# Other banks for the second token block, another order of the first drains, and two transposing chains a tick later

## The chip, the cores and the metric

The kernel runs on one core of a Trainium2 chip. The metric is the device time of one execution in microseconds (us), here the median of 3 runs. The engines are PE (TensorE), DVE (VectorE), ACT (ScalarE), POOL (GpSimd) and SP (SyncE), which issues the transfers. Each has one queue and goes through it in the order of the program; where an instruction waits, all behind it on that engine wait too.

## What is computed

A trunk of two layers over 256 tokens of width 1024, all in float32. Cut to what matters here:

```python
for l in range(2):
    x = x + 0.5 * swiglu(rms_norm(x), w1, w3, w2)          # inner width 2816
    z = rms_norm(x) @ w_in                                 # 1024 -> 6752 columns
    y_na  = neighborhood_attention(norm(na_q), norm(na_k), na_v, bias)
    y_gla = gla_bidirectional(gq, gk, gv, log_sigmoid(gfl @ up_f), log_sigmoid(gbl @ up_b))
    y_mla = softmax_attention(q from c_q, k and v from c_kv, rotary part)   # 4 heads, dense
    m = sum(sigmoid(gate_i) * (y_i @ w_br_i) for the three branches)
    x = x + m @ w_out
    x = x + 0.5 * swiglu(rms_norm(x), w1, w3, w2)
```

## The kernel before

Every float32 operand of a weight product is kept as a high and a low part in a rounded 32-bit format, and a product is three matmuls (high x high, high x low, low x high). The weights come as 212 units of up to 1 MB, in the order of use: SP brings a unit into one of three raw buffers, ACT writes its high half (L138), DVE the low half (L144), each in two pieces, into one of four buffers `hl`; then PE uses it. Products run one unit after the other, and the two token blocks of 128 tokens (t = 0 and 1) share each unit.

Two mechanisms set the order of everything. The first is `tick()`, called between bursts of matmuls: it emits the pending weight splits (`fill`) and then one step of each spawned task whose countdown has run out, in the order in which they were spawned. `spawn(gen, wait)` sets that countdown; a task is a generator, and where it yields it gives way until a later tick. So a `wait` of 1 or 2 shifts all steps of that task against the bursts, and against the steps of the other tasks, on all engines. The second is the banks of PSUM: `acc_t` gives one of four accumulator banks, `at_t` and `tr_t` one of four others (names beginning with ta); the bank released longest ago is given out first, and the first writer waits until its last reader is done.

What the change touches:

- `ffn`, the feed-forward stage, two per layer. `fform(i)` makes unit i of the first product: 32 matmuls into two acc banks, which `fdrain` empties: ACT L480 and DVE L481 add the two halves, POOL L482 multiplies by the norm's factor, ACT L487 is the Silu, DVE L489 the product, ACT L491 and DVE L493 split it. In layer 0's first stage the first two units were computed at the start, ahead of the norm's factor; they are emptied later by DVE L485 and L486, straight with the factor, at i == FIRST_R (2).
- `wide_out(first, lhs, nu, done)` is the second product, and w_out's in the mixer: for each unit and each token block a burst of 12 matmuls of 512 columns into two banks for the block (`accs[t]`), all four held to the end. The last two units are kept back, and then each of the four accumulators is finished in turn and added to x. Its first argument was not used.
- `mla_chain`, the latent attention, a task spawned among the mixer's input products with a wait of 1. Its steps are: transposes of queries and keys (L693), the rotary part, scores of heads 0 and 1 (PE, into two ta banks), their maxima (DVE L907, L908) and exponentials (ACT L915), later scores, maxima and exponentials of heads 2 and 3, the normalisation (L670, L672), transposes of the exponentials (L678), split by ACT L244 and DVE L245, and the products with the values.
- `gla_gates`, spawned behind it in the same place: log-sigmoid by ACT (exponential L968, logarithm L971, with table loads between), then for each direction DVE L978, a scan L982 and L989. `na_tr` brings transposes that DVE L710 copies.
- `mix_task(h, t)`: once the three branches of a piece are merged (DVE L1170, L1172) four transposes (L1181) and a split into the operand of w_out; spawned with a wait of 2.

Of the kernel before, what the change touches and what calls it, by code (L numbers as in the profile page):

```python
# [18 lines left out]
NCH = DFF // 256  # L19
# [9 lines left out]
FIRST_R = 2  # L29
# [16 lines left out]
def body(tc, T):  # L46
# [3 lines left out]
    with ctx:  # L50
# [18 lines left out]
        acc_t = lambda: bank("acc", 4)  # L69
        tr_t = lambda: bank("ta", 4)  # L70
        at_t = lambda: bank("ta", 4)
# [109 lines left out]
        def tick(fill_last=False):  # L181
            if not fill_last:
                fill()
            for tk in list(tasks):
                if tk.done:
                    continue
                tk.wait -= 1
                if tk.wait <= 0:
                    step(tk)
            if fill_last:  # L190
                fill()

        def spawn(gen, wait=1):
            tk = Task(gen, wait)
            tasks.append(tk)
            return tk
# [183 lines left out]
        def run(g):  # L380
            return spawn(g)
# [30 lines left out]
                    tick()  # L412
            return tks

        def wide_out(first, lhs, nu, done):
            accs = {}
            hold = []
            for u in range(nu):
                hl = unit()
                if u >= nu - 2:  # L420
                    hold.append((u, hl))
                    continue
                for t in range(2):
                    if u == 0:
                        accs[t] = (acc_t(), acc_t())
                    wide_burst(accs[t], lhs, u, hl, t, u == 0, False)
                    tick()
            for t in range(2):
                for h in range(2):
                    for u, hl in hold:  # L430
                        for kk in range(2):
                            a = kk * 1024 + h * 512
                            mm(accs[t][h], lhs(0, u, kk, t), hl[:, 0, a:a + 512], False, False)
                            mm(accs[t][h], lhs(0, u, kk, t), hl[:, 1, a:a + 512], False, False)
                            mm(accs[t][h], lhs(1, u, kk, t), hl[:, 0, a:a + 512], False, u == nu - 1 and kk == 1)
                    done(t, h, accs[t][h])
                    tick(True)
# [12 lines left out]
        def ffn(norms, after, prefetch, first=None, out=None):  # L450
            uT = {}

            def tform(i, hl, t):
                acc = acc_t()
                burst(acc[:, :256], X, hl, range(8), t, 256, True, True)
                s = s2((128, 128))
                if not rs_tk[t].done and t not in rs_x:
                    step(rs_tk[t])
                ACT.activation(out=s, in_=acc[:, :128], func=AF.Silu, scale=rs_x[t])
                DVE.scalar_tensor_tensor(out=s, in0=acc[:, 128:256], scalar=rs_x[t], in1=s,  # L460
                                         op0=ALU.mult, op1=ALU.mult)
                return s

            def tr_task(us):
                ps = tr_t().rearrange("p (k t n) -> p k t n", k=2, t=2)
                for t in range(2):
                    for i in range(2):
                        PE.transpose(ps[:, i, t, :], us[i, t], idt)
                for i in range(2):
                    o = uT[i] = s2((128, 2, 256), F32R)  # L470
                    split_bank(ps[:, i].rearrange("p t n -> p (t n)"), o[:, 0, :], o[:, 1, :])
                return
                yield

            def fdrain(i, a, b=None):
                g = s2((128, 2, 256))
                rb = rs_b["x"]
                if b is None:
                    for j in range(2):
                        ACT.activation(out=g[:, j, :], in_=a[j][:, 256:], func=AF.Copy)  # L480
                        DVE.tensor_tensor(out=g[:, j, :], in0=a[j][:, :256], in1=g[:, j, :], op=ALU.add)  # L481
                    POOL.tensor_tensor(out=g, in0=g, in1=rb[:, None, :].to_broadcast([128, 2, 256]), op=ALU.mult)  # L482
                    yield 1
                else:
                    DVE.tensor_tensor(out=g[:, 0, :], in0=a, in1=rb, op=ALU.mult)  # L485
                    DVE.tensor_tensor(out=g[:, 1, :], in0=b, in1=rb, op=ALU.mult)  # L486
                ACT.activation(out=g[:, 0, :], in_=g[:, 0, :], func=AF.Silu)  # L487
                yield 1
                DVE.tensor_tensor(out=g[:, 0, :], in0=g[:, 0, :], in1=g[:, 1, :], op=ALU.mult)  # L489
                o = uT[i] = s2((128, 2, 256), F32R)  # L490
                ACT.activation(out=o[:, 0, :], in_=g[:, 0, :], func=AF.Copy)  # L491
                yield 1
                DVE.tensor_tensor(out=o[:, 1, :], in0=g[:, 0, :], in1=o[:, 0, :].bitcast(F32), op=ALU.subtract)  # L493

            def fform(i):
                hl = unit()
                acc = [(at_t() if first is not None and i == 3 else acc_t()) for _ in range(2)]
                for b in range(2):
                    o = acc[b].rearrange("p (w t n) -> p w t n", w=2, t=2)
                    for k in range(8):  # L500
                        a = k * 256 + b * 128
                        both = xT[:, :, :, k, :].rearrange("p t w n -> p w t n")
                        mm(o, hl[:, 0, a:a + 128], both, k == 0, False)
                        mm(o[:, 0], hl[:, 1, a:a + 128], xT[:, :, 0, k, :], False, k == 7)
                    if b == 0:
                        tick()
                if i == (FIRST_R if first is not None else 2):
                    rs_bcast()
                    if first is not None:
                        for j in range(2):  # L510
                            drains[j] = run(fdrain(j, first[j][0][:, :256], first[j][1][:, :256]))
                        for j, a in held:
                            drains[j] = run(fdrain(j, a))
                if "x" in rs_b:
                    drains[i] = run(fdrain(i, acc))
                else:
                    held.append((i, acc))
                tick()

            us, drains, held = {}, {}, []  # L520
            if first is None:
                h2 = [unit(), unit()]
                for t in range(2):
                    finish(norms[t, 0])
                    finish(norms[t, 1])
                    for i in range(2):
                        us[i, t] = tform(i, h2[i], t)
                        tick(t == 0)
                utr = spawn(tr_task(us), 2)
            for i in range(2, NB):  # L530
                fform(i)
                if i == 4:
                    prefetch()
                    if first is not None:
                        load_consts()
                    if first is None:
                        finish(utr)

            def lhs(hl, u, kk, t):
                if 2 * u + kk in drains:  # L540
                    finish(drains.pop(2 * u + kk))
                return uT[2 * u + kk][:, hl, t * 128:t * 128 + 128]

            def done(t, h, acc):
                w = 512 if out is None else 256
                for a in range(0, 512, w):
                    sl = slice(h * 512 + a, h * 512 + a + w)
                    DVE.scalar_tensor_tensor(out=x[:, t, sl], in0=acc[:, a:a + w], scalar=0.5, in1=x[:, t, sl],  # L548
                                             op0=ALU.mult, op1=ALU.add)
                    if out is not None:  # L550
                        nc.sync.dma_start(out=out[t * 128:(t + 1) * 128, sl], in_=x[:, t, sl])
                if out is None:
                    after(t, h)

            wide_out(True, lhs, NCH, done)


        def mixer(l, norms, after, prefetch):
# [546 lines left out]
            u_tk = []  # L1105
# [1 line left out]
            nq = dense8(512, ev_nqk("q"))  # L1107
            q_tk = spawn(na_tr("q", nq), 3)
            dense8(512, ev_copy(gvt), between=up_proj(1, 512, ev_ukv, u_tk))
            mla_tk = spawn(mla_chain(u_tk), 1)  # L1110
            gl_tk = spawn(gla_gates(), 1)
            nk = dense8(512, ev_nqk("k"))
            k_tk = spawn(na_tr("k", nk), 2)
# [38 lines left out]
            mixed, mt = {}, {}  # L1152

            def branch(i, key):
                lh = lambda hl, k, t: yT[key, k // 2][hl][:, (k % 2) * 256 + t * 128:(k % 2) * 256 + t * 128 + 128]
                for h in range(2):
                    hl = unit()
                    for t in range(2):
# [12 lines left out]
                            e = DVE if i == 2 else POOL  # L1171
                            e.tensor_tensor(out=m, in0=m, in1=g, op=ALU.add)  # L1172
                        if i == 2:
                            mt[h, t] = spawn(mix_task(h, t), 2)
                        tick()

            def mix_task(h, t):
# [19 lines left out]
            def done(t, h, acc):  # L1197
                sl = slice(h * 512, h * 512 + 512)
                DVE.tensor_tensor(out=x[:, t, sl], in0=acc, in1=x[:, t, sl], op=ALU.add)
                after(t, h)  # L1200
            wide_out(True, lhs, 4, done)


        def spawner(ap, into, params_of=None):
# [144 lines left out]
```

## Time and profile before

| | |
|---|---|
| median of 3 runs | 1257.57 us (1257.17 to 1257.95) |
| the profiled execution | 1257.95 us |
| its span | 1256.2 us |
| PE busy | 1240.7 us, 99% of the span |
| DVE busy | 895.1 us, 71% |
| ACT busy | 712.6 us, 57% |
| POOL busy | 220.5 us, 18% |
| granted clock of TensorE, mean | 1.0 |

The span is the time from the first to the last instruction in the profile; the execution is 1.75 us longer. The views used further down are the list of what PE waits for, and stretches of the timeline, in which neighbouring instructions of one kind stand in one row. A row gives the start and the duration of the group, and in brackets how long the engine was idle before it and what released it.

### The profile page before, as it was taken

The numbers are of one execution on the slowest core, as the hardware profiler recorded it, in microseconds if no ns is written. First come the engines' busy times: TensorE is split into PE (matmuls) and PEld (weight loads), VectorE is DVE, ScalarE is ACT, GpSimd is POOL, SyncE is SP. The second block draws the span as 40 slices with busy tenths as digits, with TensorE's granted clock in tenths as the row PEclk, the third lists the DMA queues.
The fourth block names the chain that finished last, engine by engine and source line by source line (L and its number), as shares of the span: only waits on it lengthen the run. The fifth ranks groups of instructions, "written<-read, shape, count | busy, mean of one in ns | idle before, by whom it ended". The sixth has DMA issues, their size and how long they took to land.

```text
span 1256.2 us, 18300 instructions
## 1 busy us (share of the span) xinstructions
PE 1240.7 (99%) x7108; PEld 1069.0 (85%) x7108; DVE 895.1 (71%) x1386; ACT 712.6 (57%) x1315; POOL 220.5 (18%) x169
## 2 busy tenths in 40 slices
PE   7999999999999999999999999999999999999998
PEld 7888788889988898888898888888899788988887
DVE  5888736679766868887378886475896667788862
ACT  6556535657665465565365655355686644665541
POOL 0322101132011112220012220021322020122200
PEclk9999999999999999999999999999999999999999
DMA  8655644562543545556346556346535434555560
GB/s 303 210 188 201 232 170 158 174 223 92 197 167 135 201 169 172 197 191 244 135 170 223 189 183 243 122 164 245 172 101 200 163 135 169 200 197 177 196 234 34
DMA packets 37944, 228.60 MB, mean 182 GB/s; under 512 B 5777, under 2 KB 6929, under 8 KB 13281
## 3 DMA queue, kind: packets, MB, share of 16 engines
q1 hardware_dynamic: 37680, 227.36, 51.1%
q8 instruction: 56, 0.92, 0.3%
q14 instruction: 32, 0.25, 0.1%
q0 software_dynamic: 32, 0.07, 0.0%
q10 hardware_dynamic: 144, 0.00, 0.0%
HBM read 224.26 MB, written 1.05 MB: 179 GB/s over the span
## 4 chain that ended last, share of the span: by engine, by line
PE 86%; DVE 8%; ACT 4%; DMA 1%; issue 1%; POOL 0%; DVEq 0%; SPq 0%; ACTq 0%
PE acc L370 79%; DVE hl L144 6%; PE ta L370 4%; ACT hl L138 2%; DMA raw<-in_l_f_w 1%; ACT s L480 1%; PE ta L693 1%; PE ta L261 1%; DVE s L489 1%; POOL sm L571 0%; PE ta L780 0%; DVE aT L1026 0%; PE ta L1181 0%; PE ta L678 0%; ACT aT L1025 0%
## 5 line engine op out<-in xcount | busy, mean ns | idle before, releaser
L144 DVE TENSOR_TENSOR hl<-raw,hl 128x1024 fp32r<-128x1024 f32 (+2 forms) x422 | 568.3, 1386 | 97.4 <-ACT hl L138 86.6
L138 ACT ACTIVATE hl<-raw 128x1024 fp32r<-128x1024 f32 (+2 forms) x422 | 417.2, 1041 | 105.7 <-PE acc L370 88.3
L370 PE MATMUL acc<-xT,hl 128*128 128x512 f32 (+1 forms) x2768 | 472.8, 332 | 0.9 <-DVE s L481 0.5
L370 PEld LDWEIGHTS acc<-xT,hl 128*128 128x128 f32 x2768 | 415.8, 188 | 55.2 <-DVE s L481 0.8
L370 PE MATMUL acc<-hl,xT 128*128 128x512 f32 (+2 forms) x1728 | 364.7, 366 | 0.0
L370 PEld LDWEIGHTS acc<-hl,xT 128*128 128x128 f32 x1728 | 299.8, 189 | 41.9 <-issue 2.1
L370 PE MATMUL acc<-hl,s 128*128 128x512 f32 x1344 | 310.8, 391 | 1.0 <-DVE s L481 1.0
L370 PEld LDWEIGHTS acc<-hl,s 128*128 128x128 f32 x1344 | 250.7, 188 | 53.9 <-DVE s L481 1.4
L482 POOL TENSOR_TENSOR s<-s,rsb 128x512 f32<-128x512 f32 x80 | 112.0, 1400 | 355.6 <-DVE s L481 355.6
L491 ACT ACTIVATE s<-s 128x256 fp32r<-128x256 f32 x82 | 34.2, 418 | 172.4 <-DVE s L489 172.4
L481 DVE TENSOR_TENSOR s<-acc,s 128x256 f32<-128x256 f32 x158 | 59.7, 420 | 58.6 <-ACT s L480 58.6
L571 POOL TENSOR_TENSOR sm<-sm,mhalf 128x4 f32<-128x4 f32 (+2 forms) x24 | 35.9, 1494 | 198.8 <-DVE sm L575 197.3
L282 POOL TENSOR_TENSOR sm<-sm,mhalf 128x1 f32<-128x1 f32 x12 | 14.1, 1177 | 296.4 <-DVE sm L281 296.4
L480 ACT ACTIVATE s<-acc 128x256 f32<-128x256 f32 x158 | 50.7, 372 | 0.0
L245 DVE TENSOR_TENSOR s<-ta,s 128x512 fp32r<-128x512 f32 (+1 forms) x46 | 26.6, 604 | 23.9 <-ACT s L244 23.7
L244 ACT ACTIVATE s<-ta 128x512 fp32r<-128x512 f32 (+1 forms) x46 | 22.9, 531 | 35.8 <-PE ta L693 16.3
L264 ACT ACTIVATE xT<-ta,gain 128x128 fp32r<-128x128 f32 x80 | 22.9, 370 | 33.9 <-PE ta L261 33.9
L370 PE MATMUL ta<-s,s 64*64 64x128 f32 (+4 forms) x720 | 39.5, 263 | 2.4 <-ACT s L1035 2.4
L370 PEld LDWEIGHTS ta<-s,s 64*64 64x64 f32 (+3 forms) x720 | 31.7, 145 | 11.5 <-issue 5.9
L487 ACT ACTIVATE s<-s 128x256 f32<-128x256 f32 x82 | 34.2, 419 | 11.1 <-POOL s L482 0.2
L548 DVE SCALAR_TENSOR_TENSOR x<-acc,x 128x512 f32<-128x512 f32 (+1 forms) x20 | 11.3, 580 | 39.7 <-PE acc L370 39.7
L493 DVE TENSOR_TENSOR s<-s,s 128x256 fp32r<-128x256 f32 x82 | 34.0, 416 | 1.9 <-ACT s L491 1.9
(159 smaller groups left out, 648.5 us busy)
## 6 DMA issues: line engine op xcount, KB each, us to landing
raw<-in_l_f_w SPq DMA_DIRECT2D x130, 1024.0 KB, 4.9
raw<-in_l_in_g SPq DMA_DIRECT2D x16, 816.0 KB, 4.4
raw<-in_l_in_late SPq DMA_DIRECT2D x8, 1024.0 KB, 4.8
raw<-in_l_out SPq DMA_DIRECT2D x8, 1024.0 KB, 4.9
raw<-in_l_in_m SPq DMA_DIRECT2D x4, 1024.0 KB, 4.8
raw<-in_l_in_gr SPq DMA_DIRECT2D x4, 1024.0 KB, 4.9
raw<-in_l_in_r SPq DMA_DIRECT2D x4, 1024.0 KB, 4.8
raw<-in_l_in_nv SPq DMA_DIRECT2D x4, 1024.0 KB, 5.5
```

The source lines that it names most:

```text
L138: ACT.activation(out=hls[j][:, 0, sl], in_=raws[j][:, sl], func=AF.Copy)
L144: DVE.tensor_tensor(out=hl[:, 1, sl], in0=r[:, sl], in1=hl[:, 0, sl].bitcast(F32), op=ALU.subtract)
L244: ACT.activation(out=hi, in_=ps, func=AF.Copy)
L245: DVE.tensor_tensor(out=lo, in0=ps, in1=hi.bitcast(F32), op=ALU.subtract)
L370: PE.matmul(out=out, lhsT=lhsT, rhs=rhs, start=start, stop=stop, skip_group_check=True)
L480: ACT.activation(out=g[:, j, :], in_=a[j][:, 256:], func=AF.Copy)
L481: DVE.tensor_tensor(out=g[:, j, :], in0=a[j][:, :256], in1=g[:, j, :], op=ALU.add)
L482: POOL.tensor_tensor(out=g, in0=g, in1=rb[:, None, :].to_broadcast([128, 2, 256]), op=ALU.mult)
L487: ACT.activation(out=g[:, 0, :], in_=g[:, 0, :], func=AF.Silu)
L491: ACT.activation(out=o[:, 0, :], in_=g[:, 0, :], func=AF.Copy)
L493: DVE.tensor_tensor(out=o[:, 1, :], in0=g[:, 0, :], in1=o[:, 0, :].bitcast(F32), op=ALU.subtract)
L571: POOL.tensor_tensor(out=r[:, :n], in0=ss[:, :n], in1=mhalf[:, :n], op=ALU.pow)
```

## The change

It consists of four edits. The allocator of the second block's accumulators becomes an argument of `wide_out`: the feed-forward stages pass `at_t`, the mixer `acc_t` as it was. At i == FIRST_R the first drains run in the order 1, 2, 0 instead of 0, 1, 2. The latent attention is spawned with a wait of 2 instead of 1, in both layers. The mix transposes are spawned with a wait of 3 instead of 2. Line numbers of the changed file are one higher from the end of `fform` on.

```diff
-        def wide_out(first, lhs, nu, done):
+        def wide_out(bank1, lhs, nu, done):
...
                     if u == 0:
-                        accs[t] = (acc_t(), acc_t())
+                        accs[t] = (bank1(), bank1()) if t else (acc_t(), acc_t())
...
                 if i == (FIRST_R if first is not None else 2):
                     rs_bcast()
                     if first is not None:
-                        for j in range(2):
-                            drains[j] = run(fdrain(j, first[j][0][:, :256], first[j][1][:, :256]))
+                        drains[1] = run(fdrain(1, first[1][0][:, :256], first[1][1][:, :256]))
                         for j, a in held:
                             drains[j] = run(fdrain(j, a))
                 if "x" in rs_b:
                     drains[i] = run(fdrain(i, acc))
                 else:
                     held.append((i, acc))
+                if first is not None and i == FIRST_R:
+                    drains[0] = run(fdrain(0, first[0][0][:, :256], first[0][1][:, :256]))
                 tick()
...
-            wide_out(True, lhs, NCH, done)
+            wide_out(at_t, lhs, NCH, done)
...
-            mla_tk = spawn(mla_chain(u_tk), 1)
+            mla_tk = spawn(mla_chain(u_tk), 2)
...
-                            mt[h, t] = spawn(mix_task(h, t), 2)
+                            mt[h, t] = spawn(mix_task(h, t), 3)
...
-            wide_out(True, lhs, 4, done)
+            wide_out(acc_t, lhs, 4, done)
```

What it moves, at three places. The first is DVE in layer 0's mixer, at the maxima of heads 0 and 1 (L907 and L908 before, L908 and L909 after; L1127 is the product that empties the linear attention's queries, L144 a weight split). Before:

```order
L907 TENSOR_REDUCE sm_2695<-ta_2669 128x2
L908 TENSOR_SCALAR sm_2695<-sm_2695 128x2
L907 TENSOR_REDUCE sm_2698<-ta_2670 128x2
L908 TENSOR_SCALAR sm_2698<-sm_2698 128x2
L640 TENSOR_SCALAR sm_2639<-sm_2639,sm_1817 128x8
L642 TENSOR_TENSOR s2_2713<-acc_2474,sm_2639 128x512
L1127 TENSOR_TENSOR s2_2739<-acc_2641,rsb_1967 128x512
L144 TENSOR_TENSOR hl_2666<-raw_2471,hl_2666 128x816 x2
```

After:

```order
L245 TENSOR_TENSOR s2_2657<-ta_2651,s2_2656 128x512
L245 TENSOR_TENSOR s2_2666<-ta_2660,s2_2665 128x512
L641 TENSOR_SCALAR sm_2621<-sm_2621,sm_1817 128x8
L643 TENSOR_TENSOR s2_2673<-acc_2474,sm_2621 128x512
L1128 TENSOR_TENSOR s2_2699<-acc_2623,rsb_1967 128x512
L144 TENSOR_TENSOR hl_2648<-raw_2471,hl_2648 128x816 x2
L908 TENSOR_REDUCE sm_2731<-ta_2705 128x2
L909 TENSOR_SCALAR sm_2731<-sm_2731 128x2
L908 TENSOR_REDUCE sm_2734<-ta_2706 128x2
L909 TENSOR_SCALAR sm_2734<-sm_2734 128x2
```

The maxima went from ahead of the product and the weight split to behind them, and the split of the rotary part (L245) stands ahead of all.

The second is the same engine a little later, at the maxima of heads 2 and 3 (ta_2783 and ta_2784 before, ta_2826 and ta_2827 after). Before:

```order
L907 TENSOR_REDUCE sm_2809<-ta_2783 128x2
L908 TENSOR_SCALAR sm_2809<-sm_2809 128x2
L907 TENSOR_REDUCE sm_2812<-ta_2784 128x2
L908 TENSOR_SCALAR sm_2812<-sm_2812 128x2
L978 SCALAR_TENSOR_TENSOR s2_2545<-s2_2545,s2_2628 128x512
L982 SCALAR_TENSOR_TENSOR s2_2628<-s2_2823,s2_2545 128x512
L989 TENSOR_TENSOR s2_2545<-s2_2628 128x512
L710 COPY s2_2834<-ta_2829 128x512
L1127 TENSOR_TENSOR s2_2860<-acc_2755,rsb_1967 128x512
L144 TENSOR_TENSOR hl_2780<-raw_2518,hl_2780 128x816 x2
```

After:

```order
L979 SCALAR_TENSOR_TENSOR s2_2523<-s2_2523,s2_2610 128x512
L983 SCALAR_TENSOR_TENSOR s2_2610<-s2_2783,s2_2523 128x512
L990 TENSOR_TENSOR s2_2523<-s2_2610 128x512
L711 COPY s2_2794<-ta_2789 128x512
L1128 TENSOR_TENSOR s2_2820<-acc_2747,rsb_1967 128x512
L144 TENSOR_TENSOR hl_2772<-raw_2512,hl_2772 128x816 x2
L908 TENSOR_REDUCE sm_2852<-ta_2826 128x2
L909 TENSOR_SCALAR sm_2852<-sm_2852 128x2
L908 TENSOR_REDUCE sm_2855<-ta_2827 128x2
L909 TENSOR_SCALAR sm_2855<-sm_2855 128x2
```

The maxima now follow the first direction's decay product, scan and difference (L979, L983, L990), the copy, the product and the weight split, which all followed them before. PE, which reads what comes of the maxima, at that place. Before:

```order
L693 MATMUL ta_2829<-idt_77,s2_2632 128x128 x2
L693 MATMUL ta_2829<-idt_77,s2_2713 128x128 x2
L370 MATMUL acc_2755<-xT_78,hl_2560 128x256 x24
L678 MATMUL ta_2874<-idt_77,s2_2701 128x128 x4
L678 MATMUL ta_2883<-idt_77,s2_2705 128x128 x4
L693 MATMUL ta_2895<-idt_77,s2_2632 128x128 x2
L693 MATMUL ta_2895<-idt_77,s2_2713 128x128 x2
L370 MATMUL acc_2902<-hl_2666,xT_78 128x408 x12
```

After:

```order
L694 MATMUL ta_2869<-idt_77,s2_2614 128x128 x2
L694 MATMUL ta_2869<-idt_77,s2_2673 128x128 x2
L370 MATMUL acc_2876<-hl_2648,xT_78 128x408 x12
L679 MATMUL ta_2901<-idt_77,s2_2737 128x128 x4
L679 MATMUL ta_2910<-idt_77,s2_2741 128x128 x4
L370 MATMUL acc_2877<-hl_2648,xT_78 128x408 x12
```

The transposes of the first exponentials stood behind 24 matmuls of 256 columns and now stand behind twelve of 408. ta_2883 reuses the bank of ta_2783, ta_2910 that of ta_2826.

The third place is PE at the first unit of the second product in layer 0's first feed-forward stage, where block 0's burst ends and block 1's begins. Before:

```order
L370 MATMUL acc_1353<-hl_1267,s2_369 128x512
L370 MATMUL acc_1354<-hl_1267,s2_369 128x512
L370 MATMUL acc_1372<-hl_1267,s2_366 128x512
L370 MATMUL acc_1373<-hl_1267,s2_366 128x512
L370 MATMUL acc_1372<-hl_1267,s2_366 128x512
```

After:

```order
L370 MATMUL acc_1353<-hl_1267,s2_366 128x512
L370 MATMUL acc_1354<-hl_1267,s2_366 128x512
L370 MATMUL ta_1372<-hl_1267,s2_370 128x512
L370 MATMUL ta_1373<-hl_1267,s2_370 128x512
L370 MATMUL ta_1372<-hl_1267,s2_370 128x512
```

Block 1 writes two ta banks instead of two acc banks; the order of the matmuls is the same.

## Rows read from the trace of the kernel before

**Rows 1.** What PE waits for: engine, line, releaser, total us, times, longest

```profile
PE ta L370 <- ACT hl L339: 6.7, 2, 6.2
PE ta L370 <- ACT s L1035: 2.4, 2, 1.2
PE acc L370 <- DVE s L481: 1.5, 2, 1.0
...
PE ta L1181 <- DVE s L1172: 0.4, 2, 0.2
```

**Rows 2.** Timeline at the first drains (start, us, engine, line; brackets: idle before)

```profile
32.18 2.20 POOL L482 TENSOR_TENSOR s<-s,rsb 128x512 f32<-128x512 f32 x1 [9.00 <-DVE s L481]
...
33.15 1.85 DVE L489 TENSOR_TENSOR s<-s 128x256 f32<-128x256 f32 x2
...
45.07 1.19 PE L370 MATMUL acc<-xT,hl 128*128 128x512 f32 x5 [0.49 <-DVE s L481]
```

**Rows 3.** Timeline, PE, second product of the first feed-forward stage

```profile
139.49 3.80 PE L370 MATMUL acc<-hl,s 128*128 128x512 f32 x15 [1.02 <-DVE s L481]
```

**Rows 4.** Timeline, PE and DVE, mix transposes of layer 0

```profile
418.01 0.63 PE L1181 MATMUL ta<-idt,s 128*128 128x128 f32 x4 [0.20 <-DVE s L1172]
...
428.33 1.28 DVE L245 TENSOR_TENSOR xT<-ta,xT 128x512 fp32r<-128x512 f32 x2
```

**Rows 5.** Timeline, PE, latent attention among the products of layer 0

```profile
295.83 6.02 PE L370 MATMUL acc<-xT,hl 128*128 128x256 f32 x48
301.69 2.51 PE L370 MATMUL ta<-s,s 128*128 128x256 f32 x24
...
304.55 3.12 PE L370 MATMUL acc<-xT,hl 128*128 128x256 f32 x24
307.50 1.04 PE L678 MATMUL ta<-idt,s 128*128 128x128 f32 x8
...
308.90 4.72 PE L370 MATMUL acc<-hl,xT 128*128 128x408 f32 x24
```

**Rows 6.** Timeline, DVE, the same stretch

```profile
296.08 0.68 DVE L907 TENSOR_REDUCE sm<-ta 128x2 f32<-128x512 f32 x1
...
297.98 0.23 DVE L640 TENSOR_SCALAR sm<-sm 128x8 f32<-128x8 f32 x1 [0.22 <-POOL sm L571]
...
299.62 1.92 DVE L144 TENSOR_TENSOR hl<-raw,hl 128x816 fp32r<-128x816 f32 x2
...
304.23 0.69 DVE L907 TENSOR_REDUCE sm<-ta 128x2 f32<-128x512 f32 x1 [1.74 <-PE ta L370]
...
305.83 0.69 DVE L978 SCALAR_TENSOR_TENSOR s<-s,s 128x512 f32<-128x512 f32 x1
...
309.68 1.92 DVE L144 TENSOR_TENSOR hl<-raw,hl 128x816 fp32r<-128x816 f32 x2
```

**Rows 7.** Timeline, ACT, the same stretch

```profile
297.06 0.47 ACT L915 ACTIVATE s<-ta,sm 128x256 f32<-128x256 f32 x1 [1.19 <-DVE sm L908]
...
298.87 0.64 ACT L967 ACTIVATE s<-s 128x512 f32<-128x512 f32 x1
...
300.20 1.28 ACT L971 ACT_TABLE_LOAD   x1
301.49 1.34 ACT L971 ACTIVATE s<-s,ones 128x512 f32<-128x512 f32 x2
...
305.20 1.28 ACT L915 ACT_TABLE_LOAD   x1 [0.82 <-DVE sm L908]
...
307.41 0.47 ACT L915 ACTIVATE s<-ta,sm 128x256 f32<-128x256 f32 x1
```

**Rows 8.** Timeline, DVE, the same place in layer 1

```profile
924.62 0.69 DVE L907 TENSOR_REDUCE sm<-ta 128x2 f32<-128x512 f32 x1 [1.75 <-PE ta L370]
```

**Rows 9.** Windows, PE: stretch, length, busy us (matmuls), granted clock, DMA share, GB/s

```profile
6.10:9.10 3.00, 2.92 (x12) 1.00 1.01 366
10.00:12.00 2.00, 2.00 (x18) 1.00 1.02 367
```

## The prediction

> **What bounds the kernel now.** I read the idle time of TensorE first. Its waits [rows 1] add up to some 12 us of a span of 1256.2 us, and 6.7 of these lie at the start, before the first weights are there. So this is a kernel of one full engine: nothing that ACT, DVE, POOL or a transfer does counts unless TensorE stops for it. What remains is short: 2.4 us at two places in the gated linear attention (L1035), which no edit touches; 1.5 us on accumulators that DVE's L481 has still to empty, at 45.07 (0.49) and at 139.49 (1.02); and 0.4 us on the merged rows of L1172, 0.2 in each layer, the first at 418.01. Three of the four edits aim at these 1.9 us; all four together can win no more than that from stalls. The second thing to read is therefore where TensorE does *not* wait now but only just: a reordering can lose there far more than 1.9 us.
>
> **Edit 1, second token block's accumulators in the other banks.** The order shows it: at the first unit of w2 the matmuls of block 1 write ta instead of acc. At 139.49 TensorE waits 1.02 us because DVE empties the acc pair of the last w13 unit that late [rows 3]; block 0's pair had been free and ran at once. The ta banks hold nothing at that time, since the transposes that use them come only at the end of w2. The wait goes whole: 1.0 us. Behind it no wait takes its place, because the next thing block 1 needs is the same split weight that block 0 has just used. In the other three feed-forward stages TensorE does not wait at this place (two L481 waits in all, [rows 1]), so nothing is won there. Priced from both sides: 1.0 to 1.2 won (the restart has cost a little beside the wait), I take 1.0.
>
> **Edit 2, order of the first drains.** The same instructions run; the drain with a POOL multiply now starts second and block [0] last. In the trace POOL's multiply took 2.20 us at 32.18 and the two DVE products beside it 1.85 us, about 0.9 each [rows 2]. Starting POOL earlier moves it out from under part of these products, and L489 of unit 2 now stands one L493 further ahead on DVE. ACT's copy of the next unit waits for just that product, and the chain from there to 45.07 is one after the other (DVE L489, ACT L491, ACT L480, DVE L481), so the gain arrives: 0.4 of the 0.49 us. The bounds are 0 and 0.5. The cover of block [0]'s late drain is that its banks are not written again until the w2 stage.
>
> **Edit 4, mix transposes one tick later.** The wait of 0.20 us at 418.01 [rows 4] goes in both layers, because a burst of twelve 512-column matmuls now stands between L1172 and the transposes. What is moved is four PE transposes with one ACT and one DVE split. The splits move too: the DVE split of the second transposed tile comes behind two halves of a weight split, where at 428.33 the splits of two other tiles stand now, 1.28 us [rows 4], and block 1 of w_out's first unit needs it. With the wait gone and one group of transposes fewer ahead (0.47, below) it would be done some 0.7 us earlier than the first of those, near 428.3, and the matmul that needs it, the fifth of its burst, comes up near 428.2. So 0 to 0.2 us per layer may come back. Net of both layers: 0 to 0.4 won, I take 0.4.
>
> **Edit 3, latent attention one tick later.** Nothing in the waits of before [rows 1] stands for it: no gain. Its cost has to be found by going through the new order with the durations of the old one. On before's clock, in layer 0:
>
> TensorE. The scores of heads 0 and 1 ended where a run of 48 256-column matmuls begins, at 295.83. They now come one half unit of 24 later; the run took 301.69 - 295.83 = 5.86, so half is 2.93 [rows 5], and the scores end at 298.8. Then come, by the new order: 24 matmuls 2.95 (304.55 to 307.50), four transposes 0.47 (a third of the twelve from 307.50 to 308.90), 24 matmuls 2.95, the scores of heads 2 and 3 with four transposes 2.86 (301.69 to 304.55), twelve gate matmuls of 408 columns 2.36 (half of 4.72), and the four transposes of the first exponentials 0.47. That is 12.1: TensorE stands before the second group of transposes of exponentials, into ta_2910, at 310.8. That bank held the scores of heads 2 and 3, and is free when ACT has taken their exponentials. In the trace of before the same release came where the third activation begins, 307.41 [rows 7], and TensorE came to that group at 307.50 + 0.47 = 307.97: the cover was half a microsecond.
>
> DVE and ACT. Two changes in DVE's order matter. The first maxima (L908 in the new file, L907 in the old) stood at 296.08, ahead of the q product L1127 and the split L144; now they stand behind both. L144 began at 299.62 and took 1.92 [rows 6], so the maxima begin at 301.5, or 302.1 if DVE waits a little for the rotary part's split, which now stands ahead of it. ACT's exponentials began 0.98 after the maxima (297.06 - 296.08) and took 1.81 (to 298.87); then the logarithm's table 1.28 and one L971, 0.67 (half of 1.34) [rows 7]. Sum 4.8: the decay product L979 of the gated attention can begin at 306.3 to 306.9. Second change: the maxima of heads 2 and 3 were first in line at 304.23, and DVE was idle for 1.74 us ahead of them; in the new order they stand *behind* L979, the scan, L990, a copy, a product and two halves of a weight split. That row of work ran from 305.83 to 309.68 + 1.92 = 311.6 [rows 6], 5.7 us. So the maxima begin at 312.0 to 312.6. From there the table load began 0.97 later (305.20 - 304.23), and the second activation was done 2.21 after that (to 307.41) [rows 7]: 315.2 to 315.8. TensorE has stood since 310.8: **a new stall of 4.4 to 5.0 us**, on a matrix engine that is in order, so every later matmul goes with it. I take 4.6. Layer 1 has the same rows 620.4 us later, DVE's maxima at 924.62 with an idle time of 1.75 [rows 8], so 9.2 in all. The moved steps issue no DMA; SP's queue is not touched, and POOL's share of the normalisation goes along, off the path. After the stall ACT and DVE have caught up and I find no further wait up to the neighbourhood attention; nothing gives it back either, since the later waits of 2.4 us hang on TensorE's own results.
>
> On the two table loads in that chain: the rows have 1.28 us from load to first use, 300.20 to 301.49 [rows 7]. The Trainium skill (ScalarE: Activation LUTs, What ACT_TABLE_LOAD costs) counts a drain of about 1.38 us beside each load; with two loads per layer its sum would be an estimated 5.5 us more. The trace does not show that drain, and the row is taken.
>
> **Sum.** 9.2 - 1.0 - 0.4 - 0.4 = +7.4 us. The profiled execution took 1257.95, 0.38 above the median, so it would be 1265.35, and the median 1257.57 + 7.4 = 1265.0.
>
> **Rivals.** (a) *DVE reaches the first maxima as soon as the scores are there* (298.8, not 301.5 to 302.1), because the q product and the split ahead of it run earlier than I place them: the accumulator of that product is complete earlier in the new order, and the DVE queue has little idle time but some. Then the chain is 2.7 to 3.3 shorter, the stall about 1.7 per layer, and the sum 3.4 - 1.8 = +1.6: 1259.2, not slower in a measurable way. It decides from a stall under 2.15 us per layer on. Against it: L640, ahead of both in the old order and in the new, waited for POOL until 297.98 [rows 6], and no edit makes POOL earlier. (b) *No new stall at all*: exponentials come in time and only the gains are left, -1.8: 1255.8 with all of them, a little below 1255 if the feed-forward gains are larger. For that the chain would have to be 4.4 us shorter, as long as the whole row of the scan and split; I see no such room. (c) *The clock falls in the new pause.* After 6.2 us without matmuls at the start [rows 1], 12 matmuls of 256 columns took 2.92 us, where 18 took 2.00 a little later [rows 9]: half speed, 1.2 against 2.4 GHz by the spacing, though the granted clock reads 1.00 in both stretches. If as many run at the lower speed after each pause, each costs 2.92 - 12 x 0.111 = 1.6 us, 3.2 in all: 1268.2. The pauses of before are 1.2 us at most after the start, and none shows it. The Trainium skill (TensorE: Matmul & The Clock Gate, The HAM clock gate) says the same of an idle array, that it drops to the lower clock and has to earn the higher one back; by that rule the sum would be that of (c) if a pause is long enough for it, which no row here shows.
>
> **How the numbers follow.** The forecast, a stall of 4 to 5.3 us per layer at full clock: 0.60. (c): 0.17. (a) and partial stalls: 0.14. (b): 0.09. The predicted time is 1265.0. The forecast's own bounds: 8.8 to 10.0 for the stalls, 0.8 to 2.1 for the gains (edits 2 and 4 at nothing or whole, edit 1 at 1.0 to 1.2), so +6.7 to +9.2, 1264 to 1267. Down to 1259 takes in most of (a), up to 1269 takes in (c). Below 1259 lies (b) and a little of (a), above 1269 a few hundredths. A measurement of this kernel tells about 0.2%, 2.5 us, from no change: faster is (b) in its larger part, 0.07; same is most of (a) with the rest of (b), 0.11; slower is the rest, 0.82.
>
> **What would show it.** In the profile of the changed kernel, a wait of TensorE's L679 for ACT's L916, once per layer, 4 to 5 us, near 311 and 936; on DVE L908 behind a weight split, after 312 (on this clock); no L481 wait at the first w2 unit; the one at 45 shorter than 0.2; no wait of L1182 for L1173, possibly one of 0.1 on L245 just behind. I would be wrong if L908 of heads 2 and 3 began before 310, or if the stall were there and the end did not move: then something later had room that I have not seen. Half as many matmuls per microsecond behind the new wait would be (c).

## The result, and the profile after

| | before | after |
|---|---|---|
| median of 4 runs | 1257.65 us | 1270.25 us (1269.47 to 1271.0) |
| ratio, 95% interval | | 1.0099, 1.0088 to 1.0111 |
| the profiled execution, its span | 1257.95, 1256.2 | 1269.47, 1267.7 |
| granted clock of TensorE, mean | 1.0 | 0.994 |

The change makes the kernel slower by 12.6 us, 1.0%. The forecast was +7.4, 1265.0, in a range up to 1269: the sign is right, the size is not, and the time lies 1.25 us above the range.

What TensorE waits for now (engine, line, releaser, total us, times, longest), to be held against [rows 1]:

```profile
PE ta L679 <- ACT s L916: 9.9, 2, 5.0
PE ta L370 <- ACT hl L339: 6.2, 1, 6.2
PE ta L370 <- ACT s L1036: 2.4, 2, 1.2
PE ta L694 <- DVE s L829: 0.5, 2, 0.2
```

The L481 waits and the wait of the mix transposes are gone, as forecast; the new one, L679 for L916, stands once in each layer with 4.97 us. The timeline of PE around it in layer 0 (start, duration, idle time before):

```profile
307.21 0.64 PE L679 MATMUL ta<-idt,s 128*128 128x128 f32 x4
312.82 1.12 PE L679 MATMUL ta<-idt,s 128*128 128x128 f32 x4 [4.97 <-ACT s L916]
313.59 6.50 PE L370 MATMUL acc<-hl,xT 128*128 128x408 f32 x24
```

The third row is the surprise. The same 24 gate matmuls took 4.72 us before [rows 5], and the four transposes 0.6. The windows over the pause (stretch, length, PE busy and matmuls, granted clock, DMA share, GB/s) say why:

```profile
307.00:309.00 2.00, 0.85 (x7) 1.00 0.00 0
309.00:311.00 2.00, 0.00 (x0) 0.92 0.25 42
311.00:313.00 2.00, 0.18 (x1) 0.50 0.85 339
313.00:315.00 2.00, 2.00 (x8) 0.50 0.12 44
315.00:317.00 2.00, 2.00 (x7) 0.50 0.00 0
317.00:319.00 2.00, 2.00 (x11) 0.87 0.00 0
319.00:321.00 2.00, 2.00 (x16) 1.00 0.51 131
```

The granted clock falls from 1.00 to 0.50, from 2.4 to 1.2 GHz, while the engine stands, and comes back only some 4.7 us after it has gone on (by the share at 0.50 of the window from 317 to 319): 8 and 7 matmuls in 2 us, where the filled kernel further down runs 13 of the same matmuls in as long at 1.00. Layer 1 has the same: 0.50 from 940 to 944, and the 24 matmuls take 6.62 us.

Comparing the start of the same matmul in the two traces gives the ledger. The two executions already differ by 1.78 us at 26 us, where nothing is edited (in the one before, TensorE waited at three more places for the first split weights, between 13 and 16 us), so this part is chance. From there on:

| where | after less before, us |
|---|---|
| first drains, 45 us | -0.33 |
| first unit of the second product, 139 us | -1.46 |
| a transpose waiting for L829, 269 us | +0.2 |
| scores of heads 0 and 1, a wait for a DVE split, layers 0 and 1 | +0.3 each |
| the pause with its restart, layers 0 and 1 | +5.1 each |
| matmuls at the lower clock, layers 0 and 1 | +2.2 and +2.3 |
| mix transposes, layers 0 and 1 | -0.2 each |

That is +15.3 in the latent attention and -2.0 elsewhere: +13.3 with equal starts, against the 12.6 of the medians.

### The profile page after: what moved, and what is told of

Read it like the earlier page. It is cut to its first block, busy times and chain, and to the rows that moved or that the text cites. A ratio compares the mean times of both kernels' runs of the same rounds, so it can differ in the third digit from the quotient of the medians.

```text
span 1267.7 us, 18299 instructions
## 1 busy us (share of the span) xinstructions
PE 1245.0 (98%) x7108; PEld 1073.7 (85%) x7108; DVE 895.2 (71%) x1386; ACT 712.3 (56%) x1315; POOL 220.4 (17%) x169
## 4 chain that ended last, share of the span: by engine, by line
PE 91%; DVE 4%; ACT 3%; POOL 1%; issue 1%; DMA 0%; DVEq 0%; ACTq 0%; POOLq 0%
PE acc L370 75%; PE ta L370 14%; DVE hl L144 2%; POOL sm L572 1%; ACT hl L138 1%; PE ta L694 1%; PE ta L261 1%; ACT s L916 0%; PE ta L781 0%; DVE aT L1027 0%; DVE s L643 0%; PE ta L679 0%; DMA gcol<-in_gcol 0%; PE ta L1182 0%; DVE sm L637 0%
## 5 line engine op out<-in xcount | busy, mean ns | idle before, releaser
L144 DVE TENSOR_TENSOR hl<-raw,hl 128x1024 fp32r<-128x1024 f32 (+2 forms) x422 | 568.7, 1387 | 96.1 <-ACT hl L138 85.5
L370 PE MATMUL acc<-hl,xT 128*128 128x512 f32 (+2 forms) x1728 | 369.4, 369 | 0.0
L370 PEld LDWEIGHTS acc<-hl,xT 128*128 128x128 f32 x1728 | 303.1, 191 | 42.5 <-issue 2.1
L370 PE MATMUL acc<-hl,s 128*128 128x512 f32 x816 | 194.2, 390 | 0.0
L370 PEld LDWEIGHTS acc<-hl,s 128*128 128x128 f32 x816 | 152.3, 188 | 32.1 <-issue 0.7
L370 PE MATMUL ta<-hl,s 128*128 128x512 f32 (+1 forms) x624 | 148.0, 386 | 0.0
L370 PEld LDWEIGHTS ta<-hl,s 128*128 128x128 f32 x624 | 116.2, 188 | 22.5
L481 DVE TENSOR_TENSOR s<-acc,s 128x256 f32<-128x256 f32 x158 | 59.7, 420 | 59.0 <-ACT s L480 59.0
L245 DVE TENSOR_TENSOR s<-ta,s 128x512 fp32r<-128x512 f32 (+1 forms) x46 | 26.7, 605 | 41.5 <-ACT s L244 41.5
```

The costliest lines, as they stand in the source:

```text
L144: DVE.tensor_tensor(out=hl[:, 1, sl], in0=r[:, sl], in1=hl[:, 0, sl].bitcast(F32), op=ALU.subtract)
L245: DVE.tensor_tensor(out=lo, in0=ps, in1=hi.bitcast(F32), op=ALU.subtract)
L370: PE.matmul(out=out, lhsT=lhsT, rhs=rhs, start=start, stop=stop, skip_group_check=True)
```

## Experiments

**The latent attention alone.**

```diff
-            mla_tk = spawn(mla_chain(u_tk), 1)
+            mla_tk = spawn(mla_chain(u_tk), 2)
```

> The kernel before with the latent attention spawned one tick later and nothing else. Theory (the later latent attention alone makes the loss: a wait of 5.0 us, 0.3 us more at the scores, and about 2.3 us of matmuls at the lower clock behind the wait, 7.6 to 7.7 in each layer): about +15.3, near 1273, the wait of L679 for L916 5.0 us twice and a granted clock near 0.5 behind it. Rival (the later latent attention costs only its wait of 5.0 per layer, the rest of the loss comes from the other edits): +10, near 1267.7, and no fall of the clock.

Measured: 1272.1 (1270.5 to 1272.33) against 1257.86, ratio 1.0111 (1.0097 to 1.0125). That is +14.2, near the 15.3 of the theory and away from the rival's 10. The wait stands there unchanged (waits of PE, then three windows of layer 0):

```profile
PE ta L678 <- ACT s L915: 9.9, 2, 5.0
...
313.00:315.00 2.00, 0.48 (x2) 0.87 0.92 369
315.00:317.00 2.00, 2.00 (x8) 0.50 0.03 8
317.00:319.00 2.00, 2.00 (x10) 0.78 0.00 0
```

The clock fell here some 2 us later in the pause than in the changed kernel and stood at 0.50 for about half as long (by the shares of the windows at 0.50), and by the same ledger layer 0 lost 6.9 us where the changed kernel lost 7.6: the price of the fall varies from one execution to the next.

**The other three edits without it.**

```diff
-            mla_tk = spawn(mla_chain(u_tk), 2)
+            mla_tk = spawn(mla_chain(u_tk), 1)
```

> The changed kernel with the latent attention back at its old tick: the other three edits alone. Theory: they only win, 0.35 at the first drains, 1.45 at the first w2 unit and 0.2 in each layer at the mix transposes, so -2.2, near 1255.4, granted clock 1.00 everywhere. Rival (they carry part of the loss): +2 to +3, near 1260.

Measured: 1255.82 (1254.79 to 1256.39), ratio 0.9983 (0.9974 to 0.9992), -2.0 us, clock 1.0. This is the version that is faster than both kernels. With the +14.2 of the latent attention alone, the two parts add up to +12.2, against the 12.6 of the whole change. Its timeline shows edits 1 and 4 as they were forecast: block 1 writes ta with no wait before it, and so do the mix transposes, whose rows of before stand in [rows 3, 4]:

```profile
137.40 2.88 PE L370 MATMUL ta<-hl,s 128*128 128x512 f32 x12
...
418.51 0.60 PE L1182 MATMUL ta<-idt,s 128*128 128x128 f32 x4
```

**Each of the three alone.** The banks, the drains and the mix transposes, each put into the kernel before by itself:

```diff
-                        accs[t] = (acc_t(), acc_t())
+                        accs[t] = (bank1(), bank1()) if t else (acc_t(), acc_t())
...
-            wide_out(True, lhs, NCH, done)
+            wide_out(at_t, lhs, NCH, done)
...
-            wide_out(True, lhs, 4, done)
+            wide_out(acc_t, lhs, 4, done)
```

> The kernel before with only the second block's accumulators in ta banks. Theory: the wait of 1.0 us at the first w2 unit is gone with some slower matmuls behind it, 1.45 in all, the wait of 0.49 at the first drains stays: 1256.3. Rival (a bank that is missing later, at the transposes at the end of w2, gives it back): 1257.8.

```diff
-                        for j in range(2):
-                            drains[j] = run(fdrain(j, first[j][0][:, :256], first[j][1][:, :256]))
+                        drains[1] = run(fdrain(1, first[1][0][:, :256], first[1][1][:, :256]))
...
+                if first is not None and i == FIRST_R:
+                    drains[0] = run(fdrain(0, first[0][0][:, :256], first[0][1][:, :256]))
```

> The kernel before with only the other order of the first drains. Theory: the wait at 45 falls from 0.49 to 0.08, 0.35 to 0.4 won: 1257.4, no more than the measurement can just tell. Rival (what is won is taken by the wait at the first w2 unit, which is still there): 1257.8.

```diff
-                            mt[h, t] = spawn(mix_task(h, t), 2)
+                            mt[h, t] = spawn(mix_task(h, t), 3)
```

> The kernel before with only the mix transposes one tick later. Theory: the wait of L1181 for L1172 goes, and 0.1 comes back at the first w_out unit: 0.2 in each layer, 1257.4. Rival (the splits that come later cost as much): 1257.8.

Measured against 1257.72: the banks 1256.06, ratio 0.9986 (0.9977 to 0.9995), so -1.7 and clear; the drains 1257.41, 0.9999 (0.9990 to 1.0008); the mix transposes 1257.22, 0.9997 (0.9988 to 1.0006). The last two can't be told from nothing by their times. Their waits can be. The waits of PE for L481 in the kernel with the banks:

```profile
PE acc L370 <- DVE s L481: 0.5, 1, 0.5
```

In the kernel with the drains, where the mix transposes still wait:

```profile
PE acc L370 <- DVE s L481: 1.2, 1, 1.2
...
PE ta L1182 <- DVE s L1173: 0.4, 2, 0.2
PE ta L781 <- POOL s L775: 0.3, 1, 0.3
```

Of the two L481 waits, the banks take away the one of 1.0 and leave 0.5; the drains take away the one of 0.5, and the other grows from 1.0 to 1.2, so part of that gain is handed on. The rest does not reach the end either: held against the kernel before, matmul by matmul, this execution gains 0.5 us at the first drains and gives back 0.15 at 139 us, 0.2 at the transposes for L829 and, at L781, 0.3 and 0.4 in the two layers. In the kernel with the mix transposes both stay, and the L1181 row is gone from the list. The three together (-2.0) are in line with the sum of the single ones (-2.5) within the measurement; most of it is the banks, and that the drains add anything at the end is not shown.

**The pause filled with unread work.** Forty matmuls of 256 columns into a free bank stand ahead of the second group of transposes; their result is read by nobody.

```diff
+                            if h == 1:
+                                fl = acc_t()[:, :256].rearrange("p (t n) -> p t n", t=2)
+                                for k in range(40):
+                                    mm(fl, xT[:, 0, 0, k % 8, :], xT[:, :, 0, k % 8, :], k == 0, k == 39)
                             PTs[h] = p_trans(Ps.pop(h))
```

> The changed kernel with 40 matmuls of 256 columns, whose result nobody reads, set into the pause ahead of the second group of transposes, in both layers. The dependence stays as it is; only TensorE isn't idle. Theory (the array's clock falls because of the pause): 40 x 0.113 = 4.5 us of the pause are filled, the wait that is left is about 0.5, and the gate matmuls behind it start 0.19 apart instead of 0.34: 2.2 to 2.3 us less in each layer, near 1265.7, although work is added. Rival (the slow matmuls behind the wait come from weights or from ports that ACT and DVE use at that time): the pause is filled but they stay 0.34 apart, 1270.

Measured: 1268.23 (1267.21 to 1268.62), ratio 1.0082 (1.0068 to 1.0095): 2.0 us *less* than the changed kernel, with 80 matmuls more. PE in layer 0:

```profile
308.46 5.03 PE L370 MATMUL acc<-xT 128*128 128x256 f32 x40
313.68 0.66 PE L679 MATMUL ta<-idt,s 128*128 128x128 f32 x4 [0.19 <-ACT s L916]
314.09 4.72 PE L370 MATMUL acc<-hl,xT 128*128 128x408 f32 x24
...
336.20 0.66 PE L781 MATMUL ta<-idt,s 128*128 128x128 f32 x4 [0.88 <-POOL s L775]
```

The gate matmuls take 4.72 us again, to the digit of [rows 5], and the granted clock is 1.00 throughout: it was the idle array, not the weights or a port, that made them slow. But less than half of the 4.5 us came home. The last row tells where most of the rest went: 22 us later a transpose of the neighbourhood attention waits for POOL's L775, which goes back to DVE, and DVE waits for the bias (DVE in the same run):

```profile
331.73 0.29 DVE L746 CUSTOM_DVE_ANT_0 s<-ta,s 128x128 f32<-128x128 f32 x1 [3.33 <-DMA s<-in_l_bias]
```

SP issues that bias behind weight units that wait for a raw buffer (SP in the same run):

```profile
299.81 27.19 SPq L124 DMA_DIRECT2D raw<-in_l_in_g  x4
327.09 0.86 SPq L722 DMA_DIRECT2D s<-in_l_bias  x2
```

The same place in the kernel before (DVE, POOL and PE):

```profile
327.61 0.29 DVE L745 CUSTOM_DVE_ANT_0 s<-ta,s 128x128 f32<-128x128 f32 x1 [4.34 <-DMA s<-in_l_bias]
...
331.10 1.04 POOL L774 TENSOR_TENSOR s<-s,sm 128x512 f32<-128x512 f32 x1 [17.34 <-DVE sm L772]
...
332.20 0.66 PE L780 MATMUL ta<-idt,s 128*128 128x128 f32 x4
```

POOL was done at 332.14 and the transpose began at 332.20: that place had no room at all, and no list of waits of the kernel before shows it. It is also where the kernel with the drains alone loses part of its gain. In the changed kernel POOL was done at 336.42 and the transpose began at 336.48: the slow matmuls held TensorE back by just so much that it did not wait there. So of the 2.2 us per layer at the lower clock, about 0.9 would have been lost anyway.

**Half of the filling.** The same with 18 of them.

```diff
-                                for k in range(40):
+                                for k in range(18):
-                                    mm(fl, xT[:, 0, 0, k % 8, :], xT[:, :, 0, k % 8, :], k == 0, k == 39)
+                                    mm(fl, xT[:, 0, 0, k % 8, :], xT[:, :, 0, k % 8, :], k == 0, k == 17)
```

> As the kernel with the filled pause, with 18 of the unread matmuls in place of 40: at 0.125 us each they fill 2.25 us, and about 2.8 us of the pause stay empty. Theory (the clock falls for the long pause of 5 us only): granted clock 1.00, gate matmuls 0.19 apart, a time like that of the filled one, 1268.2. Rival (a pause of some 3 us is already enough): clock 0.5 behind the wait and about 1270.

Measured: 1271.26 (1268.72 to 1273.27), ratio 1.0107 (1.0091 to 1.0124). Neither expectation holds as it stands. The windows of layer 0, then of layer 1:

```profile
311.00:313.00 2.00, 0.00 (x0) 1.00 0.83 248
313.00:315.00 2.00, 1.63 (x11) 1.00 0.41 170
...
339.00:341.00 2.00, 2.00 (x8) 0.50 1.06 341
...
942.00:944.00 2.00, 0.87 (x5) 0.76 0.75 313
944.00:946.00 2.00, 2.00 (x8) 0.50 0.00 0
```

In layer 0 TensorE stood for 2.83 us and the clock stayed up; in layer 1 it stood as long and the clock fell. And in layer 0 the clock fell later all the same, behind another pause:

```profile
337.49 0.66 PE L781 MATMUL ta<-idt,s 128*128 128x128 f32 x4 [2.49 <-POOL s L775]
337.91 3.59 PE L370 MATMUL acc<-hl,xT 128*128 128x408 f32 x12
```

Here the bias came 1.3 us later than in the run with 40 (DVE's L746 at 333.01, against 331.73), and the wait at L781 was 2.49 us. So a pause of 2.83 us went either way, one of 2.49 us was followed by a fall, and the bias is a second place that can make one. In layer 0 that wait and the slow matmuls behind it cost 4.0 us, more than the 2.2 of the fall that was spared.

**The gates of the linear attention one tick later too.**

```diff
-            gl_tk = spawn(gla_gates(), 1)
+            gl_tk = spawn(gla_gates(), 2)
```

> The changed kernel with the gates of the linear attention also spawned one tick later, so that on DVE the maxima of heads 2 and 3 stand ahead of the decay product and the scan again. Theory (the new wait is DVE's order alone): the maxima begin about 305.4 instead of 309.5, the exponentials need no table load between, the wait of L679 is under 0.3 and the clock stays up: near 1255.5. Rival (the wait comes from the bank and from the scores being later, whatever stands on DVE): a wait of 2 to 5 us stays, 1262 to 1270.

Measured: 1264.01 (1263.43 to 1266.27), ratio 1.0053 (1.0041 to 1.0066). In three of the five executions, the profiled one among them, the mean clock was 1.0; in the two others, at 1265.17 and 1266.27, it was 0.997, so the clock fell in them somewhere. My theory in this form fell, and the time lies in the rival's range: the scan stands behind the maxima again, and still the wait is 2.13 us. PE, DVE and ACT:

```profile
292.51 0.66 PE L694 MATMUL ta<-idt,s 128*128 128x128 f32 x4 [1.32 <-DVE s L245]
312.50 0.66 PE L679 MATMUL ta<-idt,s 128*128 128x128 f32 x4 [2.13 <-ACT s L916]
...
307.33 1.92 DVE L144 TENSOR_TENSOR hl<-raw,hl 128x816 fp32r<-128x816 f32 x2
309.16 0.69 DVE L908 TENSOR_REDUCE sm<-ta 128x2 f32<-128x512 f32 x1
...
310.13 1.28 ACT L916 ACT_TABLE_LOAD   x1 [1.15 <-DVE sm L909]
```

The maxima still stand behind the weight split, and the logarithm, which now comes later, still puts a table load in front of the exponentials. A new wait of 1.3 us came up earlier, where the rotary transposes meet a bank that DVE has not emptied yet. I had named one row of the queue as the cause; the others count as well.

**Only the weight split put behind the maxima.**

```diff
-                tick()
+                tick(nm == "k")
             na_tk = spawn(na_chain([q_tk, k_tk]), 4)
```

> The changed kernel with one thing moved: in the tick of the second scores the weight split (L144, two halves, 1.9 us) is emitted behind the tasks' steps, so that on DVE the maxima of heads 2 and 3 stand ahead of it. Theory (the wait is the time that the row ahead of the maxima takes on DVE): the maxima begin 1.84 us earlier, at 307.65 on the clock of the changed kernel, the wait of L679 falls from 4.97 to about 3.1; -3.7 at the same fall of the clock, near 1266.5, and near 1264 if the clock stays up in the shorter pause. Rival (the wait is set by the scores and the table load, the row on DVE only fills the time): wait unchanged, 1270.

Measured: 1265.59 (1264.31 to 1267.86), ratio 1.0067 (1.0052 to 1.0082). DVE's maxima and PE's wait in layer 0:

```profile
307.83 0.68 DVE L1128 TENSOR_TENSOR s<-acc,rsb 128x512 f32<-128x512 f32 x1
308.43 0.68 DVE L908 TENSOR_REDUCE sm<-ta 128x2 f32<-128x512 f32 x1
...
311.76 0.66 PE L679 MATMUL ta<-idt,s 128*128 128x128 f32 x4 [3.13 <-ACT s L916]
312.17 6.25 PE L370 MATMUL acc<-hl,xT 128*128 128x408 f32 x24
```

The two traces stand 0.80 us apart here, so the maxima began at 307.63 on the clock of the changed kernel, as expected. The wait fell from 4.97 to 3.13, by 1.84, just the time that the split took on DVE: for this split, the wait is the work that stands ahead of the maxima on DVE. For the rest of that row (L979 to L1128) it is argued from the durations, since no run moves it and nothing else. The clock fell behind 3.13 us too (6.25 instead of 4.72), though at a lower price than in the changed kernel, where the 24 matmuls took 6.50.

**Another bank for the waiting transposes.** The second group of transposes goes to a free acc bank.

```diff
-            def p_trans(P):
-                ps = tr_t().rearrange("p (b t n) -> p b t n", b=2, t=2)
+            def p_trans(P, bk=tr_t):
+                ps = bk().rearrange("p (b t n) -> p b t n", b=2, t=2)
...
-                            PTs[h] = p_trans(Ps.pop(h))
+                            PTs[h] = p_trans(Ps.pop(h), acc_t if h == 1 else tr_t)
```

> The changed kernel with the second group of transposes of exponentials written to an acc bank, which is free, in place of the bank that heads 2 and 3 still hold. Theory (TensorE is stopped by a row of work on DVE and ACT that is late as a whole; the bank is only where it meets it first): the transposes run at once, but the products with the values, 4.6 us later, need splits that stand on ACT and DVE behind the exponentials of heads 2 and 3; a wait of 3.4 to 4.0 us comes there instead, 1266 to 1269. Rival (the reuse of the bank alone is the cause): the wait is gone and comes back nowhere, 1256.

Measured: 1267.51 (1267.01 to 1268.59), ratio 1.0082 (1.0067 to 1.0097). The transposes run at once, and TensorE stands 8 us later:

```profile
308.16 0.60 PE L679 MATMUL acc<-idt,s 128*128 128x128 f32 x4
308.51 4.71 PE L370 MATMUL acc<-hl,xT 128*128 128x408 f32 x24
316.24 0.39 PE L370 MATMUL ta<-s,s 128*128 128x256 f32 x1 [3.01 <-ACT s L244]
316.96 2.27 PE L370 MATMUL ta<-s,s 128*128 128x256 f32 x11 [0.34 <-DVE s L245]
```

Together 3.35 us, where 3.4 to 4.0 were expected. The reuse of the bank is only where TensorE meets the late chain first; give it another bank and it meets it at the products with the values.

## Why the prediction was wrong in size

*Edits 1, 2 and 4.* Right at their places within half a microsecond. Forecast -1.0, -0.4 and -0.4; in the profile -1.46, -0.33 and -0.4, together -2.0 by the experiment without edit 3. Edit 1 won more than its bounds of 1.0 to 1.2: the wait alone had been counted, while the matmuls at the restart and behind it had been later by another 0.4. For edit 2, "so the gain arrives" holds up to 45 us; in the traced execution of the kernel with the drains alone, later waits took it back.

*Edit 3, the wait.* The mechanism, its place and its size were right. The steps of the working can be checked one by one. The two traces stand 3.03 us apart there, so this goes on the times of the changed kernel's rows:

```profile
298.81 0.68 DVE L908 TENSOR_REDUCE sm<-ta 128x2 f32<-128x512 f32 x1
...
303.79 0.69 DVE L979 SCALAR_TENSOR_TENSOR s<-s,s 128x512 f32<-128x512 f32 x1 [1.44 <-ACT s L972]
...
309.49 0.68 DVE L908 TENSOR_REDUCE sm<-ta 128x2 f32<-128x512 f32 x1
...
312.66 0.47 ACT L916 ACTIVATE s<-ta,sm 128x256 f32<-128x256 f32 x1
```

The first maxima began at 301.8 on the clock of before (forecast 301.5 to 302.1), L979 at 306.8 (306.3 to 306.9), the second maxima at 312.5 (312.0 to 312.6), and the second activation was done, by the start of the third as in the forecast, at 315.7 (315.2 to 315.8); TensorE stood from 310.9 (310.8). Each is near the late end of its range, so the wait was 4.97 with 0.16 at the restart, against bounds of 4.4 to 5.0 and the 4.6 that I took: 1.1 us more over both layers. That DVE had to wait for the rotary split was named as the condition of the late end; the same split also held the scores up by 0.3 in each layer, which the sum left out.

*Edit 3, the clock.* This is the step that failed: the sum, "9.2 - 1.0 - 0.4 - 0.4", has no term for the clock, so that the matmuls behind the new wait were taken at full speed. The fall of the clock stood among the rivals, (c), with a chance of 0.17 and 1.6 us a pause; it came in both layers and cost 2.2 and 2.3. The chance was too low because the trace of before has no pause between 1.2 and 6.2 us, and I took the lack of a row for a reason against it; the one row that did bear on it, the half speed behind the pause of 6.2 us [rows 1, 9], spoke for it. The price was too low because I carried over the number of slow matmuls from the start, twelve of 256 columns; here it was four transposes and a dozen matmuls of 408. The Trainium skill (TensorE: Matmul & The Clock Gate, The HAM clock gate) says that an idle array drops to the lower clock; the pauses of 3.0 us and more agree with it without exception, and the traced ones of 2.13 show no fall.

*What lies behind.* "I find no further wait" holds for the changed kernel only because its slow matmuls held TensorE back; for the kernel of the forecast, at full clock, it was wrong: with the pause filled, L781 waits 0.88 and 0.95 us in the two layers. SP's order is as it was ("SP's queue is not touched"), but the bias that it brings set the pace at L781 already before, with no room; it took nearly half of what the clock gave back when the pause was filled.

*The sum.* 2 x 5.1 for the pauses, 2 x 0.3 for the scores, 4.5 for the clock, less 2.0, make 13.3 with equal starts; the medians have 12.6. Even (c), 1268.2, was too low, by the 1.1 of the pauses, the 0.6 of the scores and the price of the clock.

## What to carry to other kernels

Where one engine is busy for 99% of the time, look in the trace for the places where it is released half a microsecond early, not for those where it waits: a reordering that puts a few rows of another engine ahead of such a release can cost their full length, and here the length could be added up from the old trace, 4.6 us for a wait and restart of 5.1. To that sum belongs what a pause does to TensorE's clock: here every pause of 3 us or more was followed by half-speed matmuls that cost 1.5 to 2.8 us, and forty unread matmuls in the pause were cheaper than the pause, while eighteen were not. And take parts of a change apart: three of these four edits together win 2 us, and the fourth loses 14.

## What the runs showed of the hardware

The granted clock against the pause ahead of it, in the profiled executions: 1.2 us (before, at L1035) and 2.13 us (both layers of the kernel with the later gates) 1.00; 2.83 us once 1.00 and once 0.50 in one execution; 2.49 us at L781 0.50; 3.13 us and 3.0 us (the other bank, with 0.34 more behind one matmul in layer 0), two pauses each, and 4.97 us, four pauses, 0.50. Two executions of the kernel with the later gates that were not traced have a mean clock of 0.997, so it fell in them as well; how long their pauses were is not known.

The fall need not come while the engine stands: behind the wait of 2.49 us at 337.49 the window from 337 to 339 still reads 0.97, and behind that of 3.01 us at 316.24 the one from 315 to 317 reads 1.00 and the next 0.63. Whether the clock falls behind 2.1 to 2.8 us, and what decides it, stays open, as does why the bias took 1.6 us longer from SP's issue to DVE's L746 in one run (326.77 to 333.01, against 327.09 to 331.73).

At the start of the program the granted clock reads 1.00 where 12 matmuls took 2.92 us [rows 9], so there the column does not show the level that the spacing shows; the trace's record of the clock begins only at 10.19 us, and the column counts what lies ahead of it as 1.00.

From the start of ACT's table load at 310.45 to the first exponential at 311.74, in the changed kernel, it was 1.29 us, as in [rows 7], where ACT's instruction ahead of the load at 300.20 had ended at 300.18; the Trainium skill's further 1.38 us for a drain (ScalarE: Activation LUTs, What ACT_TABLE_LOAD costs) does not show.
